# One conditioning row per stretch of half steps: moving w_ada passes on VectorE, and four more SwiGLU pairs transposed by DMA

## The chip, the cores and the metric

The kernel runs on one core of a Trainium2 chip. The metric is the device time of one execution in microseconds, as a median of several runs; the kernel before takes 2384.58 us (three runs, 2383.78 to 2389.31).

## The reference, cut to what matters

One decoder layer over 256 tokens of width 2048, in float32:

```python
mod = (silu(c) @ w_ada + b_ada).reshape(9, 2048)       # conditioning: shift, scale, gate, three times
h = modulate(rms_norm(x, norm_ffn1), mod[0], mod[1])
x = x + 0.5 * mod[2] * swiglu(h, w_ffn1_gu, w_ffn1_down)         # d_ff 5632
h = modulate(rms_norm(x, norm_mix), mod[3], mod[4])
x = x + mod[5] * token_mixing(h, w_in, w_ret_branch, w_swa_branch, w_out, sinks)
h = modulate(rms_norm(x, norm_ffn2), mod[6], mod[7])
x = x + 0.5 * mod[8] * swiglu(h, w_ffn2_gu, w_ffn2_down)
return rms_norm(x, norm_final)
# token_mixing: h @ w_in (13312 columns) -> retention q, k, v, g | window attention q, k, v | two branch gates
#   out = (sigmoid(gate_ret) * (ro @ w_ret_branch) + sigmoid(gate_swa) * (so @ w_swa_branch)) @ w_out
```

The nine rows of `mod` are 9 x 2048 dot products of length 2048 with `silu(c)`. They are worked out on VectorE beside the matmuls of the layer.

## The kernel before, in words

**Products.** Every large matrix product is done on TensorE with float32 split into a high and a low part, three terms each: high by high, low by high, high by low (lines 338, 339 and 341). A weight block of four k-tiles by 512 columns (1 MB) is loaded by SyncE into a `raw` tile. It is used in two *half steps* of two k-tiles each. For a half step ScalarE casts the block's half to the high part `wh` (L351) and VectorE subtracts to get the low part `wl` (L353); then TensorE does 12 matmuls of 512 columns, for two token halves and two k-tiles. `wh` and `wl` have three buffers each (pool `wsp`), so they can be made at most three half steps ahead. Where the activations lie in float32 (the branches, the output projection and both down projections) ScalarE and VectorE also split an activation pair `a` for every two k-tiles (L386, L387).

**Raw tiles.** There are four (`RAWS = 4`). Weight blocks use them, and so do the rows of `w_ada`: a row of the conditioning is 128 outputs, a 1 MB tile of 128 by 2048.

**Conditioning.** A row is loaded (L201) and reduced in four passes of 512 columns (`ada_pass`, L206), each followed by a small read of the sum. `tick()` is called after each half step; it adds `pace["rate"]` and takes the next pass when one is due. In the mixer three outputs (7, 6 and 5: 48 rows, 192 passes) go at 0.95 passes per half step, and at 0.25 while the attention's softmax runs; in the second feed-forward output 8 (16 rows) goes at 64/160 = 0.4. A row's load is issued two passes ahead of its first. In the first feed-forward the rows go to a tile of their own (`slot`) for the most part.

**Order.** SyncE's queue follows the order of the code (`manual_schedule`), and it holds everything behind an instruction that waits, say for a free raw tile. The order on the other engines is set by the framework's scheduler at build time, except in the norm stages, which are written out by hand. `tc.issue_after(ins)` only forbids that an instruction stands ahead of `ins` on its engine.

**SwiGLU pairs.** The up projection of a feed-forward is done in eleven pairs of 512 columns (gate, up). A pair's product must be transposed. Either TensorE does it (`transpose_to`, L479, eight 128x128 transposes for a pair, copied out of PSUM at L480), or a DMA does: ScalarE takes the float32 words apart in two 16-bit planes (L496), SyncE issues a transposing DMA (L501), and ScalarE puts the planes together (L512). These three steps are generators (`later`) that advance once per weight block. In the first feed-forward the opening pairs are 0 to 7 (`EARLY = 8`); of these, pairs 1 and 5 go by DMA, and so do pairs 8 and 9; in the second, pairs 0 to 9.

**Softmax.** In the mixer, eight groups of four heads (quads) pass through `softmax_heads`, one step per weight block. ScalarE writes a quad's weights apart into `planes_of` (L1159), and four steps later SyncE issues two transposing DMAs for them (L1168), in the same queue as the weight loads.

Of the kernel before, what the change touches and what calls it, by code (L numbers as in the profile page):

```python
# [20 lines left out]
DFF = 5632  # L21
# [56 lines left out]
def layer_kernel(  # L78
# [164 lines left out]
    def conditioning(outputs, place, behind):  # L243
# [5 lines left out]
        for m, gain, row in outputs:  # L249
            sums = ada_sums()  # L250
            for k in range(KD):
                for q in range(AQ):
# [13 lines left out]
                            gate_out(m, row)  # L266
                    yield

    def gate_out(m, row):
# [77 lines left out]
    def split(pool, tag, src, n, hi_engine="act"):  # L347
        k = src.shape[1]
        hi = pool.tile([P, 2, n], F32R, tag=tag + "h", name=nm(tag + "h"))[:, :k, :]
        lo = pool.tile([P, 2, n], F32R, tag=tag + "l", name=nm(tag + "l"))[:, :k, :]  # L350
        cast.append(nc.scalar.copy(hi, src).ins)  # L351
        del cast[:-1]
        low.append(nc.vector.tensor_sub(lo, src, hi.bitcast(F32)).ins)  # L353
        del low[:-1]
        return hi, lo

    cast, low, newest = [], [], []
# [651 lines left out]
    for g, ks in enumerate(groups):  # L1009
        final = g == len(groups) - 1  # L1010
        if final:
            set_pace(ROWS_FFN1, 32 * 192 // 32, place_row, 1)
        order = chunks if (len(groups) - g) % 2 else chunks[::-1]
        coming = iter(()) if final else group(groups[g + 1])
        due = 0 if final else 2 * len(groups[g + 1])
        stay = () if final else order[-2:]
        for i, n in enumerate(order):
            visit(n, ks, n not in stay, final)
            if final:
                turn_step()  # L1020
            last = len(order) - 2
            for _ in range((i + 1) * due // last - i * due // last if i < last else i == last):
                next(coming, None)
            if n in stay:
                continue
            if not final:
                to_parts(n)
            elif n % 2:
                swiglu_up(
                    banks.pop(n - 1),  # L1030
                    banks.pop(n),
                    tiles,
                    n // 2,
                    (part_of(n - 1), part_of(n)),
                    n // 2 in (1, 5),
                )
    gate = gate_row()
    tiles.append(slot())
    row_ring.append(two_rows())
    pace["rate"] = (192 - 32) / 117  # L1040
    pace["ahead"] = AQ
    ffn_up(held, gu, tiles, EARLY, turned=range(EARLY, DFF // CH - 1))
    gate_in = gate_load(gate, 2)
    wi = w_in[0]
    held, head, ahead, *calls = into_norm(3, wi, O_SK, O_SV)
# [6 lines left out]
    soft = one.tile([P, NT * D], F32, tag="x", name="soft")  # L1052
    planes_of = one.tile([P, D], F32, tag="row", name="planes_of")
    RATE_SOFT, RATE_AFTER = 0.25, 0.95
    set_pace([(7, 2, None), (6, None, None), (5, None, 1.0)], 192 / 0.95, raw_row, 2)

    def in_chunk(c0):
        return gemm(held, wi, [c0])[0]
# [142 lines left out]
    def softmax_heads():  # L1201

        turned = {}
        for at in range(4 * (QUADS + 1) + 2):
# [15 lines left out]
        pace["rate"] = RATE_AFTER  # L1220

    for ci in range(4):
        b = in_chunk(O_SQ + ci * CH)
        work = []
        for t in range(NT):
            u = t512()
            nc.any.tensor_copy(u, b[t])
            work.append(turn_by_dma(qo[:, ci * 4 : ci * 4 + 4, t * P : (t + 1) * P], u))

        def asking(ci=ci):  # L1230
            asked.add(ci)
            if ci == 0:
                pace["rate"] = RATE_SOFT
                side.append(softmax_heads())

        soon(later(work, asking))
# [259 lines left out]
```

## Time and profile before

| what | value |
|---|---|
| median of three runs | 2384.58 us |
| profiled execution, its own time | 2393.78 us |
| its span | 2392.0 us |
| TensorE busy | 2351.4 us, 98% |
| VectorE busy | 1702.1 us, 71% |
| ScalarE busy | 1310.0 us, 55% |
| granted TensorE clock, mean | 0.997 |
| DMA queue that carries the loads (q1), share of 16 engines | 74.4% |

The page gives busy time by engine and by group of instructions. TensorE's busy time is modelled and overlaps, so the number of matmuls in a stretch of time says more than the busy share. In quiet minutes (60 us) 266 matmuls stand. The first feed-forward ends at about 760 us, the window attention's softmax runs from about 900 to 1080 us, the branch products from 1270 to 1530 us, the second feed-forward's up projection from about 1640 to 2140 us.

### The profile page before, as it was taken

Reading aid. Unit: us, or ns where it says so; the run is one execution under the profiler, and the core shown is the slowest. Engines: PE = TensorE matmul, PEld = TensorE weight load, DVE = VectorE, ACT = ScalarE, POOL = GpSimd, SP = SyncE. Lnnn points to the kernel's source line nnn. Section 1 sums busy time; section 2 is a strip of 40 time slices with the busy share of each in tenths; the row PEclk is TensorE's granted clock in tenths of the full one; section 3 lists DMA queues with packets and bytes.
Section 4 is the critical chain, followed back from the end, with each engine's and each line's share of the span. In section 5 each row is a group of like instructions: output and inputs, shape, how many; then the busy total and the mean of one; then the engine's idle time right before and its main releaser. Section 6 shows DMA issues by size and latency. Waiting matters only on the chain. (4 is left out here: it accounts for less than half of the span.)

```text
span 2392.0 us, 28418 instructions
## 1 busy us (share of the span) xinstructions
PE 2351.4 (98%) x10470; PEld 1924.5 (80%) x10470; DVE 1702.1 (71%) x2635; ACT 1310.0 (55%) x1792; POOL 7.7 (0%) x18
## 2 busy tenths in 40 slices
PE   7999999999999999999999999999999999999998
PEld 5788888888788888778887787887888888888886
DVE  6887799778877768976776676767655555545656
ACT  6553456454546568774555464466445445454544
POOL 0000000000000000000000000000000000000000
PEclk9999999999999999999999999999999999999999
DMA  9977789998876789867689797755667877765553
GB/s 354 367 278 277 265 284 342 349 339 316 321 255 236 279 270 247 253 213 286 248 278 293 236 299 282 272 195 192 237 238 237 254 247 246 255 220 194 183 204 124
DMA packets 177581, 625.78 MB, mean 262 GB/s; under 512 B 100321, under 2 KB 100705, under 8 KB 106913
## 3 DMA queue, kind: packets, MB, share of 16 engines
q1 hardware_dynamic: 175362, 613.11, 74.4%
q0 software_dynamic: 1504, 9.81, 1.0%
q8 instruction: 82, 1.34, 0.2%
q10 hardware_dynamic: 576, 1.05, 0.1%
q14 instruction: 57, 0.47, 0.1%
HBM read 597.16 MB, written 4.22 MB: 251 GB/s over the span
## 5 line engine op out<-in xcount | busy, mean ns | idle before, releaser
L351 ACT CAST wh<-raw 128x1024 fp32r<-128x1024 f32 x794 | 834.0, 1053 | 927.1 <-PE pa L339 895.4
L353 DVE TENSOR_TENSOR wl<-raw,wh 128x1024 fp32r<-128x1024 f32 x794 | 964.2, 1223 | 524.6 <-ACT wh L351 522.3
L338 PE MATMUL pa<-wh,hh 128*128 128x512 f32 x2192 | 855.4, 391 | 3.3 <-ACT wh L351 3.3
L339 PE MATMUL pa<-wh,hl 128*128 128x512 f32 x2192 | 854.5, 390 | 0.2 <-DVE hl L601 0.2
L341 PE MATMUL pa<-wl,hh 128*128 128x512 f32 x2192 | 778.2, 392 | 1.4 <-DVE wl L353 1.3
L338 PEld LDWEIGHTS pa<-wh,hh 128*128 128x128 f32 x2192 | 411.9, 188 | 93.6 <-ACT wh L351 5.3
L341 PEld LDWEIGHTS pa<-wl,hh 128*128 128x128 f32 x2192 | 409.9, 188 | 90.4 <-DVE wl L353 4.3
L339 PEld LDWEIGHTS pa<-wh,hl 128*128 128x128 f32 x2192 | 412.1, 188 | 85.2 <-DVE hl L601 0.4
L339 PE MATMUL pa<-wh,a 128*128 128x512 f32 x944 | 365.8, 390 | 0.4 <-DVE a L387 0.4
L341 PE MATMUL pa<-wl,a 128*128 128x512 f32 x944 | 351.0, 392 | 9.4 <-DVE wl L353 9.4
L338 PE MATMUL pa<-wh,a 128*128 128x512 f32 x944 | 350.7, 392 | 1.7 <-DVE t L607 1.1
L206 DVE CUSTOM_DVE_ANT_0 raw<-raw,cact 128x512 f32<-128x512 f32 (+1 forms) x296 | 189.8, 695 | 65.5 <-DMA raw<-in_w_ada_dram 59.4
L341 PEld LDWEIGHTS pa<-wl,a 128*128 128x128 f32 x944 | 177.3, 188 | 49.9 <-DVE wl L353 13.5
L338 PEld LDWEIGHTS pa<-wh,a 128*128 128x128 f32 x944 | 178.0, 189 | 40.3 <-DVE t L607 1.9
L339 PEld LDWEIGHTS pa<-wh,a 128*128 128x128 f32 x944 | 177.8, 188 | 37.9 <-DVE a L387 1.0
L206 DVE CUSTOM_DVE_ANT_0 slot<-slot,cact 128x512 f32<-128x512 f32 (+1 forms) x216 | 170.0, 835 | 5.1 <-DMA slot<-in_w_ada_dram 4.8
L512 ACT COPY slot<-back 128x512 uint16<-128x512 uint16 x124 | 82.7, 766 | 0.0
L387 DVE TENSOR_TENSOR a<-slot,a 128x512 fp32r<-128x512 f32 x118 | 80.5, 684 | 0.0
L386 ACT CAST a<-slot 128x512 fp32r<-128x512 f32 x118 | 72.7, 617 | 1.9 <-DVE t L671 1.9
L496 ACT COPY flat<-t 128x512 uint16<-128x512 uint16 x112 | 63.5, 616 | 8.1 <-DVE t L1344 5.5
L206 DVE DVE_READ_ACCUMULATOR2_ANT sums<- 128x1 f32 x512 | 42.2, 82 | 0.0
L996 DVE TENSOR_TENSOR slot<-slot,pa 128x512 f32<-128x512 f32 x48 | 31.9, 683 | 3.2 <-PE pa L341 3.1
(205 smaller groups left out, 1143.1 us busy)
## 6 DMA issues: line engine op xcount, KB each, us to landing
raw<-in_w_ffn_gu_dram SPq DMA_DIRECT2D x160, 1024.0 KB, 5.2
raw<-in_w_in_dram SPq DMA_DIRECT2D x104, 1024.0 KB, 5.7
raw<-in_w_ffn_down_dram SPq DMA_DIRECT2D x88, 1024.0 KB, 4.9
raw<-in_w_ada_dram SPq DMA_DIRECT2D x73, 1024.0 KB, 5.5
slot<-in_w_ada_dram SPq DMA_DIRECT2D x67, 1024.0 KB, 7.1
raw<-in_w_ffn_gu_dram SPq DMA_DIRECT2D x32, 512.0 KB, 5.5
raw<-in_w_swa_branch_dram SPq DMA_DIRECT2D x16, 1024.0 KB, 5.1
raw<-in_w_ret_branch_dram SPq DMA_DIRECT2D x16, 1024.0 KB, 5.0
```

The source lines that it names most:

```text
L206: nc.vector.tensor_tensor_reduce(out=w[:, at], in0=w[:, at], in1=cact[:, at], scale=1.0, scalar=0.0, op0=ALU.mult, op1=ALU.add, accum_out= ...
L338: nc.tensor.matmul(ps, ah[:, j, ts], wh[:, j, :], start=first, stop=False)
L339: nc.tensor.matmul(ps, al[:, j, ts], wh[:, j, :], start=False, stop=False)
L341: nc.tensor.matmul(ps, ah[:, j, ts], wl[:, j, :], start=False, stop=last).ins
L351: cast.append(nc.scalar.copy(hi, src).ins)
L353: low.append(nc.vector.tensor_sub(lo, src, hi.bitcast(F32)).ins)
L386: nc.scalar.copy(hi, v)
L387: nc.vector.tensor_sub(lo, v, hi.bitcast(F32))
L496: nc.scalar.copy(planes[:, i, :], words(src)[:, :, i])
L512: nc.scalar.copy(into[:, :, :, i], held["turned"][:, i])
L996: nc.vector.tensor_add(p, p, b)
```

## The change

Three things are changed.

1. The conditioning of the mixer (outputs 7, 6, 5) and of the second feed-forward (output 8) goes through a new generator, `conditioning_by_rows`. It paces rows and not passes: `share` is added per half step, and when 4 have come together the next row's load is issued. Its four passes follow in four consecutive half steps, beginning three half steps after the load (`lead=3`). Each pass is put behind a low part on VectorE: `low[0]`, the one traced before the latest, since `split` now keeps two. The shares are 0.95, 0.25 and 0.4, as the rates were.
2. Of the opening pairs, 1, 3, 5 and 7 go by DMA and not only 1 and 5.
3. The eleventh pair (number 10) goes by DMA in both feed-forwards.

```diff
+    def conditioning_by_rows(outputs, behind, lead=3):
+        sums = {}
+        coming = [(m, k, gain, row) for m, gain, row in outputs for k in range(KD)]
+        queue, now, due = [], 0, AQ
+        while coming or queue:
+            due += pace["share"]
+            if due >= AQ and coming:
+                due -= AQ
+                m, k, gain, row = coming.pop(0)
+                raw = raw_row()
+                ada_load(m, k, raw)
+                pin = behind.ins if behind is not None and now < AQ else None
+                queue.append([m, k, gain, row, raw, now + lead, 0, pin])
+            if queue and queue[0][5] <= now:
+                m, k, gain, row, raw, _, q, pin = queue[0]
+                if m not in sums:
+                    sums[m] = ada_sums()
+                with tc.issue_after(pin or low[0]):
+                    ada_pass(k, raw, sums[m], q)
+                queue[0][6] += 1
...
+            now += 1
+            yield
...
         low.append(nc.vector.tensor_sub(lo, src, hi.bitcast(F32)).ins)
-        del low[:-1]
+        del low[:-2]
...
-                    n // 2 in (1, 5),
+                    n // 2 % 2 == 1,
...
-    ffn_up(held, gu, tiles, EARLY, turned=range(EARLY, DFF // CH - 1))
+    ffn_up(held, gu, tiles, EARLY, turned=range(EARLY, DFF // CH))
...
-    set_pace([(7, 2, None), (6, None, None), (5, None, 1.0)], 192 / 0.95, raw_row, 2)
+    set_pace_by_rows([(7, 2, None), (6, None, None), (5, None, 1.0)], RATE_AFTER)
...
-    set_pace([(8, None, 0.5)], 160, raw_row, 2)
-    ffn_up(held, w_ffn2_gu[0], tiles, 0, head, range(DFF // CH - 1), ahead)
+    set_pace_by_rows([(8, None, 0.5)], 0.4)
+    ffn_up(held, w_ffn2_gu[0], tiles, 0, head, range(DFF // CH), ahead)
```

In the program as a whole TensorE has 32 transposes fewer, ScalarE has 16 copies apart (L496) and 16 copies together (L512) more, 8 copies out of PSUM (L480) and 2 others (L1197) fewer, VectorE 2 copies more, and SyncE 8 transposing DMAs more. Lines of the changed kernel lie 35 further down.

The order on VectorE in the branch products (about 1358 us of the profile before). `wl` is a low part, `a` the low half of an activation pair, and an L206 pair of rows is one pass and the read of its sum. Before, where the pass and its read stand four times in a row at the first "...":

```order
L353 TENSOR_TENSOR wl_10680<-raw_10660,wh_10679 128x1024
L206 ISA raw_10778,sums_10735<-raw_10778,cact 128x512
L206 ISA sums_10735 128x1
...
L353 TENSOR_TENSOR wl_10701<-raw_10698,wh_10700 128x1024
L387 TENSOR_TENSOR a_10657<-slot_9563,a_10657 128x512
L353 TENSOR_TENSOR wl_10720<-raw_10698,wh_10719 128x1024
L353 TENSOR_TENSOR wl_10746<-raw_10743,wh_10745 128x1024
```

The same place in the changed kernel:

```order
L388 TENSOR_TENSOR wl_10703<-raw_10700,wh_10702 128x1024
L206 ISA raw_10638,sums_9299<-raw_10638,cact 128x512
L206 ISA sums_9299 128x1
L422 TENSOR_TENSOR a_10661<-slot_9566,a_10661 128x512
L388 TENSOR_TENSOR wl_10722<-raw_10700,wh_10721 128x1024
L206 ISA raw_10638,sums_9299<-raw_10638,cact 128x512
L206 ISA sums_9299 128x1
L223 TENSOR_REDUCE modc<-sums_9299 128x16
L224 TENSOR_TENSOR modc<-modc,bcols 128x16
L388 TENSOR_TENSOR wl_10747<-raw_10744,wh_10746 128x1024
L206 ISA raw_10718,sums_10781<-raw_10718,cact 128x512
```

Four passes in one piece between two low parts have become one pass after each low part.

SyncE's loads there, first before:

```order
L328 DMA raw_10698<-in_w_ret_branch_dram 128x2048
L328 DMA raw_10743<-in_w_ret_branch_dram 128x2048
L201 DMA raw_10778<-in_w_ada_dram 128x2048
L328 DMA raw_10781<-in_w_ret_branch_dram 128x2048
L328 DMA raw_10822<-in_w_ret_branch_dram 128x2048
```

and after:

```order
L201 DMA raw_10638<-in_w_ada_dram 128x2048
L363 DMA raw_10664<-in_w_ret_branch_dram 128x2048
L363 DMA raw_10700<-in_w_ret_branch_dram 128x2048
L201 DMA raw_10718<-in_w_ada_dram 128x2048
L363 DMA raw_10744<-in_w_ret_branch_dram 128x2048
```

The new row `raw_10718` is loaded while the passes of `raw_10638` are still to come (they stand after the low parts of `raw_10664` and `raw_10700`), so two of the four raw tiles hold rows there, and the weight blocks take turns on the other two. Before, the row `raw_10778` is read in one piece, ahead of the low parts of `raw_10698` and `raw_10743`, two blocks that stand before it in the queue of loads.

ScalarE in the softmax (about 950 us), where `planes_of` is the quad's copy that the transposing DMAs wait for. Before:

```order
L351 CAST wh_7509<-raw_7507 128x1024
L1159 COPY planes_of<-soft 128x768 x4
L351 CAST wh_7526<-raw_7507 128x1024
L512 COPY slot_6360<-back_7395 128x4x128 x2
L512 COPY slot_6360<-back_7443 128x4x128 x2
L351 CAST wh_7589<-raw_7587 128x1024
```

After, a few casts further on:

```order
L386 CAST wh_7613<-raw_7595 128x1024
L531 COPY flat_7554<-t_7500 128x512 x2
L386 CAST wh_7644<-raw_7642 128x1024
L1194 COPY planes_of<-soft 128x768 x4
L531 COPY flat_7631<-t_7507 128x512 x2
L386 CAST wh_7660<-raw_7642 128x1024
L386 CAST wh_7688<-raw_7686 128x1024
```

This quad's four copies stand after the 317th weight cast before and after the 321st now, two casts ahead of that of the block `raw_7686`. On SyncE the quad's two transposing DMAs stand directly ahead of the load of `raw_7686`, as they did before. A second quad, sixteen casts later, has moved in the same way (from after the 333rd cast to after the 337th).

More of the change, by code (lines that the diff above doesn't have):

```diff
@@ L267, in conditioning, with set_pace_by_rows @@
                     yield
+    def conditioning_by_rows(outputs, behind, lead=3):
[18 more added lines that the diff above has]
+                queue[0][6] += 1
+                if q == AQ - 1:
+                    queue.pop(0)
+                    if k == KD - 1:
+                        ada_end(m, slice(0, KD), sums[m], gain)
+                        if row is not None:
+                            gate_out(m, row)
+            now += 1
+            yield
+    def set_pace_by_rows(outputs, share):
+        assert next(pace["steps"], None) is None
+        pace["steps"] = conditioning_by_rows(outputs, pace["behind"])
+        pace["rate"], pace["due"], pace["share"] = 1.0, 0.0, share
     def gate_out(m, row):
@@ L1219, in softmax_heads @@
             yield
-        pace["rate"] = RATE_AFTER
+        pace["share"] = RATE_AFTER
     for ci in range(4):
@@ L1232, in asking @@
             if ci == 0:
-                pace["rate"] = RATE_SOFT
+                pace["share"] = RATE_SOFT
                 side.append(softmax_heads())
```

## The prediction

> **What bounds the kernel now.** I read the page first, then TensorE by minutes, then what it waits for, then VectorE at one of the waits.
>
> ```profile
> PE 2351.4 (98%) x10470; PEld 1924.5 (80%) x10470; DVE 1702.1 (71%) x2635; ACT 1310.0 (55%) x1792; POOL 7.7 (0%) x18
> L351 ACT CAST wh<-raw 128x1024 fp32r<-128x1024 f32 x794 | 834.0, 1053 | 927.1 <-PE pa L339 895.4
> ```
>
> TensorE is the bound. ScalarE's weight casts idle 927.1 us, 895.4 of it until TensorE gives a buffer back: operands usually lie ready up to three half steps ahead, so only a delay longer than that lead costs time. The minutes show where this happens (after the stretch: TensorE's busy time and number of matmuls; the granted clock stands before the DMA share).
>
> ```profile
> 1260.00:1320.00 60.00, 57.57 (x250) 46.36 (x249) 41.11 (x70) 37.22 (x49) 0.00 (x0) 1.00 1.00 291
> 1320.00:1380.00 60.00, 54.94 (x224) 43.84 (x224) 43.77 (x74) 26.24 (x32) 0.00 (x0) 0.94 0.71 250
> 1380.00:1440.00 60.00, 60.00 (x266) 49.67 (x266) 45.00 (x73) 36.74 (x46) 0.00 (x0) 1.00 0.89 285
> 1440.00:1500.00 60.00, 58.17 (x257) 47.82 (x256) 38.98 (x64) 25.84 (x29) 0.00 (x0) 1.00 0.79 294
> 1500.00:1560.00 60.00, 59.45 (x262) 48.50 (x261) 42.22 (x63) 28.91 (x34) 1.05 (x2) 1.00 0.73 260
> 1860.00:1920.00 60.00, 59.74 (x264) 49.17 (x263) 32.97 (x40) 28.83 (x34) 0.00 (x0) 1.00 0.81 254
> ```
>
> A quiet minute has 266 matmuls, so one takes 60/266 = 0.2256 us and a half step of twelve 2.71 us. The two minutes of the first branch products lack 58 matmuls, those of the second 13: 71 x 0.2256 = 16.0 us. 1860 to 1920 lacks 2, 0.45 us. The waits of TensorE between 1270 and 1540 us (total, times, longest) name VectorE:
>
> ```profile
> PE pa L341 <- DVE wl L353: 8.9, 8, 2.2
> PE pa L338 <- DVE slot L1360: 0.4, 1, 0.4
> PE pa L339 <- DVE a L387: 0.4, 1, 0.4
> ```
>
> The waits are 9.7 us of the 16.0; the rest is restart and the clock, below. SyncE and VectorE ahead of the wait at 1360.9:
>
> ```profile
> 1349.35 0.33 SPq L201 DMA_DIRECT2D raw<-in_w_ada_dram  x1
> ```
>
> ```profile
> 1353.37 1.23 DVE L353 TENSOR_TENSOR wl<-raw,wh 128x1024 fp32r<-128x1024 f32 x1 [0.89 <-ACT wh L351]
> 1357.13 0.69 DVE L206 CUSTOM_DVE_ANT_0 raw<-raw,cact 128x512 f32<-128x512 f32 x1 [2.53 <-DMA raw<-in_w_ada_dram]
> ...
> 1359.59 1.22 DVE L353 TENSOR_TENSOR wl<-raw,wh 128x1024 fp32r<-128x1024 f32 x1
> 1360.72 0.68 DVE L387 TENSOR_TENSOR a<-slot,a 128x512 fp32r<-128x512 f32 x1
> 1361.33 1.22 DVE L353 TENSOR_TENSOR wl<-raw,wh 128x1024 fp32r<-128x1024 f32 x1
> ```
>
> The row lands 7.8 us after its issue. VectorE stands 2.53 us at its first pass, then does four passes (2.46 us from 1357.13 to 1359.59), and the low part that TensorE needs stands behind all of it: 6.2 us from low part to low part where TensorE uses one every 2.71.
>
> **Part 1, the passes in the mixer.** Nothing is added: the same 192 passes at 0.61 us. In the new order one pass follows each low part. Low part 1.14 us (start to start, 1359.59 to 1360.72), pass 0.61, activation pair 0.61 every second half step: 2.06 us of 2.71, so VectorE keeps up at every half step. The row's wait goes too: the load is issued three half steps ahead, and the pass stands behind low parts whose blocks are queued after the row, so the data needed next by TensorE no longer waits for a row that comes later. I take the whole 16.0 us (bounds: 9.7 if only the waits shrink, 16.0). In the second feed-forward the same gives 0.4 us, and there a row comes only every ten half steps. The mixer's last row ends some nine half steps (24 us) later than before by the order, still some eighteen ahead of the additions that need its gate: nothing waits for it.
>
> Around the first feed-forward's down projection the scheduler has moved a group of passes behind the additions that free PSUM. TensorE waited there at 645 us:
>
> ```profile
> PE pa L338 <- DVE t L607: 1.1, 2, 0.6
> ```
>
> These 1.1 us may go, but the low part behind the passes comes as late as before, so I count 0 (bounds: 1.1 us gained to 1.1 lost).
>
> The stage's clock is in those 16 us. The two stretches behind the longest waits:
>
> ```profile
> 1323.00:1326.80 3.80, 3.80 (x11) 2.94 (x12) 1.56 (x3) 1.11 (x2) 0.00 (x0) 0.57 0.91 319
> 1361.30:1364.60 3.30, 3.30 (x9) 2.61 (x8) 1.24 (x2) 0.49 (x1) 0.00 (x0) 0.52 0.94 348
> ```
>
> The clock is granted at 0.57 and 0.52 for about 3.5 us after waits of 2.0 to 2.2 us: 20 matmuls in 7.1 us, where 31 would fit, 2.5 us lost. A new wait of 2 us therefore has to be priced with up to 1.3 us on top. The Trainium skill (TensorE: Matmul & The Clock Gate, HAM oscillation) says that idle gaps over about 3.4 us are what brings the clock down; here 2.0 to 2.2 us were enough, so the measurement decides, and by the page's figure the new waits below would carry no such addition.
>
> **Part 2, the transposes.** Four pairs leave TensorE: 32 transposes. One pair on TensorE:
>
> ```profile
> 316.57 0.39 PE L338 MATMUL pa<-wh,hh 128*128 128x512 f32 x1
> 316.80 1.03 PE L479 MATMUL ps<-small_c,t 128*128 128x128 f32 x8
> 317.59 0.48 PE L341 MATMUL pa<-wl,hh 128*128 128x512 f32 x1
> ```
>
> Eight take 317.59 - 316.80 = 0.79 us of a TensorE that has no other gap there: 4 x 0.79 = 3.2 us gained. What they cost elsewhere:
>
> ```profile
> L512 ACT COPY slot<-back 128x512 uint16<-128x512 uint16 x124 | 82.7, 766 | 0.0
> L496 ACT COPY flat<-t 128x512 uint16<-128x512 uint16 x112 | 63.5, 616 | 8.1 <-DVE t L1344 5.5
> ```
>
> ```profile
> 336.19 1.69 SPq L501 DMA_TRANSPOSE back<-flat  x1
> 342.71 3.39 SPq L501 DMA_TRANSPOSE back<-flat  x1
> ```
>
> A pair takes four copies of each kind, 4 x (0.766 + 0.616) = 5.5 us on ScalarE, spread over some nine weight blocks (49 us) of an engine that is 55% busy, and holds SyncE 1.7 to 3.4 us for each tile. Pair 1 does this at 336 to 346 us without a wait of TensorE, since all loads there run ahead; the new pairs lie in the same stage, and the eleventh at the start of a down projection that needs it in its last block group, 10 x 4 half steps or 108 us later. I take 0 (bounds: 0 to 1 us a pair).
>
> **Part 3, the raw tiles.** This speaks against the change. A row now holds its raw tile from load to last pass, 3 + 4 = 7 half steps, and rows come every 4/0.95 = 4.2, so mostly two of four tiles hold rows and weight blocks take turns on two. A block's load then starts when the block before last is finished, and loop time is landing + cast + two low parts with a pass and a pair between. In the mixer from 1090 to 1540 us the median landing times are:
>
> ```profile
> raw<-in_w_in_dram SPq DMA_DIRECT2D x45, 1024.0 KB, 5.0
> raw<-in_w_ada_dram SPq DMA_DIRECT2D x35, 1024.0 KB, 6.0
> raw<-in_w_ret_branch_dram SPq DMA_DIRECT2D x15, 1024.0 KB, 5.0
> back<-flat SPq DMA_TRANSPOSE x12, 7.5
> ```
>
> The loop is 5.0 + 1.05 + 1.14 + 0.61 + 0.61 + 1.22 and about 0.1 for signals = 9.7 us for four half steps of 10.8: 1.1 us to spare, besides the lead. Single landings as long as the 7.8 us above overdraw it by 1.7 us and are made good in two loops. I take 1.5 us in all, near the median's end (bounds: 0; 71 us if every landing took 7.8, 42 loops x 1.7). The Trainium skill (DMA: Bandwidth & Descriptors, Anatomy of one DMA) fits 2.0 us + bytes/436e3, an estimate of 4.4 us for 1 MB; by it this term would be 0, the sum 1.5 us lower.
>
> **Part 4, the softmax.** Two quads' copies now stand four casts later on ScalarE, two casts ahead of a block whose load waits on SyncE behind the quad's transposes. Before, the closest case has three casts:
>
> ```profile
> 1028.06 1.06 ACT L351 CAST wh<-raw 128x1024 fp32r<-128x1024 f32 x1
> 1029.02 3.03 ACT L1159 COPY planes_of<-soft 128x768 uint16<-128x768 uint16 x4
> 1031.95 1.05 ACT L351 CAST wh<-raw 128x1024 fp32r<-128x1024 f32 x1
> 1034.80 1.06 ACT L351 CAST wh<-raw 128x1024 fp32r<-128x1024 f32 x1 [1.79 <-PE pa L339]
> 1039.80 1.05 ACT L351 CAST wh<-raw 128x1024 fp32r<-128x1024 f32 x1 [3.95 <-DMA raw<-in_w_in_dram]
> ```
>
> From the end of the first cast (1029.12) to that of the late one (1040.85) are 11.7 us. With three buffers a cast ends about 1.05 us into the half step two before its own. The cast two later must be done within 4 x 2.71 - 1.05 = 9.8 us, so TensorE waits 1.9 us; three later it was within 12.5, and it did not wait. Two places: 3.8 us (bounds: 0, if small products stretch those half steps; 6.4 with 1.3 us of half clock at each).
>
> **Sum.** 2393.78 (the profiled execution's own time; its span is 2392.0) - 16.0 - 0.4 - 3.2 + 1.5 + 3.8 = 2379.5 us. The median of the runs, 2384.58, lies 9.2 us below the profiled execution. I carry this difference over unchanged: 2370 us.
>
> **The rivals.**
> - *The two-tile loop becomes the bound* (slower). The same number of bytes moves as before, which speaks against it; that loads are no longer drawn ahead speaks for it. Without this term the gain is 19.6 - 3.8 = 15.8 us over 42 loops, 0.38 us each: the gain is gone once landings average 5.0 + 1.1 + 0.38 = 6.5 us, the row's own 6.0 not far. At 7.0 us: 42 x 0.9 = 38 us, less 15.8, 2407 us.
> - *The stalls are in part the profile's*. The difference of 9.2 us could be these very waits, longer when transfers are traced. Then the runs gain only 14.3 - 9.2 = 5.1 us: 2379.5.
> - *The wait stays.* The row still lands after its pass comes up, and VectorE stands before each low part: only the block of passes is gone. Of the 6.2 us above, 2.53 were the wait, 41%. Keeping 41% of 16.0 leaves 14.3 - 6.6 = 7.7 us: 2377, with any lateness of the loads near 2382. Against it: the load is issued 8.1 us ahead and rows have a free tile then.
>
> **How the numbers follow.** Forecast 0.70, two-tile loop 0.12, profile's stalls 0.10, the wait stays 0.08. 0.3% of 2384.58 is 7.2 us, about what a measurement of this kernel can tell from no change: faster is below 2377.4, slower above 2391.7. The forecast is faster; of the two rivals near the edge 0.03 falls there too; the rest of them, 0.15, is the same; the loop is slower. The range: without any new wait 2370 - 5.3 = 2365, and if runs lost as much again at places not counted here (3.7 us), 2361; upwards it takes in the second and third rival, to 2384, and leaves out the loop.
>
> **What would show it.** Right: in the branch stage no four passes in a row on VectorE, no wait of TensorE over 1 us, clock 1.00, 264 or more matmuls in each minute; 32 transposes at the transposing line instead of 64 in the feed-forwards; weight loads released by low parts, casts that wait for DMA for up to 1 us. Two waits of about 2 us on a cast held by a load, at about 960 and 1010 us. Wrong: casts waiting for DMA throughout 1090 to 1540 us with landings over 6.5 us; waits of VectorE for row loads still at 2 us; new waits of TensorE at 400 to 540 us behind the added transposes.

## The result, and the profile after

The changed kernel takes 2392.08 us (median, 2387.27 to 2396.61), the kernel before 2384.93 us (2383.47 to 2389.31): a ratio of 1.0027, 95% interval 1.0020 to 1.0035. It is 7.15 us slower, 0.3%, where 2370 was forecast and faster; the difference is small, but the interval of the ratio leaves out 1. The profiled execution took 2392.35 us (span 2390.6), close to its median.

The page of the changed kernel, TensorE's counts and the weight casts:

```profile
PE 2349.6 (98%) x10438; PEld 1919.6 (80%) x10438; DVE 1706.7 (71%) x2637; ACT 1322.1 (55%) x1814; POOL 7.7 (0%) x18
L386 ACT CAST wh<-raw 128x1024 fp32r<-128x1024 f32 x794 | 832.3, 1053 | 915.6 <-PE pa L374 812.1
```

32 matmul instructions are gone. Of the casts' idle time all but 812.1 us, that is 103.5 us, ends with something other than TensorE; before it was 31.7 (927.1 - 895.4). TensorE by minutes in the changed kernel (busy time and number of matmuls, granted clock, DMA share, GB/s):

```profile
600.00:660.00 60.00, 57.56 (x247) 0.97 0.77 291
840.00:900.00 60.00, 58.27 (x263) 1.00 0.89 274
900.00:960.00 60.00, 59.64 (x293) 1.00 0.71 208
960.00:1020.00 60.00, 58.45 (x287) 1.00 0.81 230
1020.00:1080.00 60.00, 57.61 (x276) 1.00 0.79 251
...
1260.00:1320.00 60.00, 58.01 (x253) 1.00 0.90 277
1320.00:1380.00 60.00, 59.39 (x260) 1.00 0.83 304
1380.00:1440.00 60.00, 58.21 (x250) 0.97 0.88 286
1440.00:1500.00 60.00, 59.78 (x264) 1.00 0.78 286
1500.00:1560.00 60.00, 59.78 (x264) 1.00 0.78 277
1860.00:1920.00 60.00, 60.00 (x267) 1.00 0.76 259
```

The minute from 1320 to 1380, at 224 matmuls and a clock of 0.94 before, is nearly full, and so is 1860 to 1920. But 1380 to 1440, full before, lacks 16, and the minutes of the softmax (960 to 1080) have 563 where the kernel before had 297 + 292 = 589. What ScalarE waits for between 1090 and 1540 us (total, times, longest):

```profile
ACT wh L386 <- PE pa L374: 147.2, 102, 2.4
ACT wh L386 <- DMA raw<-in_w_in_dram: 26.8, 8, 8.0
ACT wh L386 <- DMA raw<-in_w_swa_branch_dram: 10.0, 4, 4.0
ACT wh L386 <- DMA raw<-in_w_ret_branch_dram: 6.2, 3, 2.8
```

Casts now stand 43 us for weight loads. The same view of the kernel before names no load; there VectorE's passes waited 39.5 us for rows, and that wait is gone. The new order on VectorE is as the diff says, a pass (L206) behind each low part (L388):

```profile
1354.16 0.69 DVE L422 TENSOR_TENSOR a<-slot,a 128x512 fp32r<-128x512 f32 x1
1355.00 1.23 DVE L388 TENSOR_TENSOR wl<-raw,wh 128x1024 fp32r<-128x1024 f32 x1 [0.15 <-ACT wh L386]
1356.14 0.69 DVE L206 CUSTOM_DVE_ANT_0 raw<-raw,cact 128x512 f32<-128x512 f32 x1
```

So the trouble that was named is cured, and another has come. Where it is worst in the mixer, at 1423.4 us, SyncE's queue and the cast that TensorE then waits for read so:

```profile
1410.18 0.33 SPq L201 DMA_DIRECT2D raw<-in_w_ada_dram  x1
1410.56 5.01 SPq L536 DMA_TRANSPOSE back<-flat  x2
1415.67 1.01 SPq L363 DMA_DIRECT2D raw<-in_w_in_dram  x2
```

```profile
1422.34 2.00 ACT L386 CAST wh<-raw 128x1024 fp32r<-128x1024 f32 x2 [7.99 <-DMA raw<-in_w_in_dram]
```

A row's load and two transposing DMAs, which hold SyncE 5 us, stand ahead of two weight loads. The cast waits 7.99 us, nearly the whole lead of three half steps (8.1 us); with its own 1.05 us it takes more, and TensorE waits 1.8 us.

### The profile page after: what moved, and what is told of

The parts are those of the page before. It is cut to its first block, busy times and chain, and to the rows that moved or that the text cites. A ratio compares the mean times of both kernels' runs of the same rounds, so it can differ in the third digit from the quotient of the medians.

```text
span 2390.6 us, 28350 instructions
## 1 busy us (share of the span) xinstructions
PE 2349.6 (98%) x10438; PEld 1919.6 (80%) x10438; DVE 1706.7 (71%) x2637; ACT 1322.1 (55%) x1814; POOL 7.7 (0%) x18
## 3 DMA queue, kind: packets, MB, share of 16 engines
q10 hardware_dynamic: 576, 1.05, 0.1%
## 4 chain that ended last, share of the span: by engine, by line
PE 52%; DMA 2%; DVE 1%; ACT 1%; issue 0%; SPq 0%; DVEq 0%; ACTq 0%
PE pa L376 17%; PE pa L373 17%; PE pa L374 17%; DMA raw<-in_w_in_dram 1%; DVE wl L388 1%; ACT wh L386 1%; DMA back<-flat 0%; SPq L536 0%; PE ps L1228 0%; ACT flat L531 0%; PE pd L1327 0%; PE pd L1312 0%; PE pd L1326 0%; PE pd L1325 0%; DVE a L422 0%
## 5 line engine op out<-in xcount | busy, mean ns | idle before, releaser
L388 DVE TENSOR_TENSOR wl<-raw,wh 128x1024 fp32r<-128x1024 f32 x794 | 968.2, 1223 | 584.7 <-ACT wh L386 583.0
L386 ACT CAST wh<-raw 128x1024 fp32r<-128x1024 f32 x794 | 832.3, 1053 | 915.6 <-PE pa L374 812.1
L373 PEld LDWEIGHTS pa<-wh,hh 128*128 128x128 f32 x2192 | 411.9, 188 | 97.5 <-ACT wh L386 10.5
L206 DVE CUSTOM_DVE_ANT_0 raw<-raw,cact 128x512 f32<-128x512 f32 (+1 forms) x296 | 202.7, 693 | 10.0 <-ACT cact L173 6.1
L206 DVE CUSTOM_DVE_ANT_0 slot<-slot,cact 128x512 f32<-128x512 f32 (+1 forms) x216 | 170.0, 835 | 2.3 <-DMA slot<-in_w_ada_dram 2.2
L547 ACT COPY slot<-back 128x512 uint16<-128x512 uint16 x140 | 93.5, 766 | 0.0
L531 ACT COPY flat<-t 128x512 uint16<-128x512 uint16 x128 | 72.5, 616 | 3.8 <-DVE t L1300 3.7
L206 DVE DVE_READ_ACCUMULATOR2_ANT sums<- 128x1 f32 x512 | 42.6, 83 | 0.0
```

The lines of the kernel that those rows point to most:

```text
L206: nc.vector.tensor_tensor_reduce(out=w[:, at], in0=w[:, at], in1=cact[:, at], scale=1.0, scalar=0.0, op0=ALU.mult, op1=ALU.add, accum_out= ...
L373: nc.tensor.matmul(ps, ah[:, j, ts], wh[:, j, :], start=first, stop=False)
L531: nc.scalar.copy(planes[:, i, :], words(src)[:, :, i])
L547: nc.scalar.copy(into[:, :, :, i], held["turned"][:, i])
```

## The experiments

All of them compute the whole layer. Each is compared with runs of the kernel before on the same chip, and those medians moved by 1 us (2384.4 to 2385.3), so the table gives the difference too. The last columns count matmuls in the profiled execution. "Losses" in the expectations are worked out from the trace: the time from one 512-column matmul's start to the next matmul's beyond 0.227 us, summed where it is over 0.14 us (the next matmul may be of any size).

| kernel | median us | less before, us | 95% interval of the ratio | 960 to 1080 | 1260 to 1560 |
|---|---|---|---|---|---|
| before, the first profile | 2384.93 | 0 | | 589 | 1259 |
| before, second profile (e1) | | | | 590 | 1294 |
| changed | 2392.08 | +7.2 | 1.0020 to 1.0035 | 563 | 1291 |
| changed again (e6) | 2392.55 | +8.1 | 1.0027 to 1.0055 | 560 | 1305 |
| four pairs only (e2) | 2382.88 | -2.2 | 0.9983 to 1.0004 | 589 | 1303 |
| mixer's rows only (e3) | 2387.70 | +2.6 | 1.0002 to 1.0019 | 569 | 1310 |
| second feed-forward's rows only (e4) | 2387.86 | +2.8 | 0.9993 to 1.0014 | 590 | 1284 |
| pairs and mixer's rows (e5) | 2389.81 | +5.4 | 1.0013 to 1.0034 | 562 | 1304 |
| lead of 1 (e7) | 2381.75 | -2.7 | 0.9979 to 0.9997 | 566 | 1327 |
| lead of 5 (e8) | 2426.31 | +41.9 | 1.0169 to 1.0197 | 592 | 1183 |
| lead of 1, shift (e9) | 2381.56 | -3.8 | 0.9976 to 0.9994 | 579 | 1329 |
| shift (e10) | 2381.47 | -3.9 | 0.9976 to 0.9993 | 590 | 1315 |
| eleventh pair back (e11) | 2389.58 | +4.2 | 1.0009 to 1.0027 | 567 | 1283 |
| lead of 1, shift, pair back (e12) | 2381.02 | -4.3 | 0.9975 to 0.9992 | 578 | 1330 |
| shift in the softmax only (e13) | 2385.62 | +1.2 | 0.9993 to 1.0014 | 590 | 1296 |
| shift in the mixer only (e14) | 2387.28 | +2.9 | 1.0004 to 1.0022 | 563 | 1318 |
| shift, no added pairs (e15) | 2382.24 | -2.2 | 0.9980 to 0.9998 | 591 | 1313 |
| shift of eight (e16) | 2383.81 | -0.6 | 0.9992 to 1.0012 | 585 | 1309 |

**The kernel before, profiled once more.** No edit.

> The kernel before once more, for a second profiled execution. If the 9.2 us by which its first profiled execution lay above the median were stalls of the branch products in that one execution, the new one has fewer: own time 2383 to 2388 us, matmuls missing from the minutes 1260 to 1380 and 1440 to 1560 us at 20 to 45 and not 71, no half clock. If profiling always costs that much: own time 2392 to 2395 us and again some 70 missing.

It took 2387.34 us, in the range that meant that the first profile's stalls were in part its own. TensorE in that second profile of the kernel before:

```profile
1260.00:1320.00 60.00, 56.77 (x247) 1.00 0.99 287
1320.00:1380.00 60.00, 57.82 (x253) 1.00 0.79 283
1380.00:1440.00 60.00, 60.00 (x267) 1.00 0.88 288
1440.00:1500.00 60.00, 59.97 (x265) 1.00 0.78 288
1500.00:1560.00 60.00, 59.45 (x262) 1.00 0.72 258
```

In the four minutes of which the prediction counted 71 missing matmuls, 37 are missing here (1064 - 247 - 253 - 265 - 262): 8.3 us, and no half clock. So only about half of the 16.0 us was there to be had. Two experiments below leave the mixer as it was, e2 and e4: ScalarE, VectorE and SyncE go through the same instructions in the same order from 660 to 1560 us as in the kernel before. They lack 27 and 46 matmuls from 1260 to 1560 us, so the first profile, with 71, is the worst of four.

**The parts, one at a time.** e2 has the four pairs alone:

```diff
-                    n // 2 in (1, 5),
+                    n // 2 % 2 == 1,
...
-    ffn_up(held, gu, tiles, EARLY, turned=range(EARLY, DFF // CH - 1))
+    ffn_up(held, gu, tiles, EARLY, turned=range(EARLY, DFF // CH))
...
-    ffn_up(held, w_ffn2_gu[0], tiles, 0, head, range(DFF // CH - 1), ahead)
+    ffn_up(held, w_ffn2_gu[0], tiles, 0, head, range(DFF // CH), ahead)
```

> The kernel before with the four more pairs turned by DMA alone. Theory A (rows that hold raw tiles cost the time): 32 transposes less on TensorE, 3 us faster than before, 2382 us. Rival B (the added transposing DMAs hold SyncE and the weight loads behind them): 3 to 10 us slower than before.

2382.88 us, 2.2 less than the kernel before in that comparison, near theory A's 2382; the interval just holds no change.

e3 and e4 have `conditioning_by_rows` in the mixer alone and in the second feed-forward alone (the `set_pace_by_rows` line of the one or the other in the change's diff, no added pairs).

> The kernel before with the new generator in the mixer alone. Theory A: the whole loss lies here, 10 us slower than before (2395), casts that wait for weight loads 35 us or more between 1090 and 1540 us as in the changed kernel. Rival B: no slower than before, 2380 to 2385.

> The kernel before with the new generator in the second feed-forward alone. There weight loads keep three tiles or more, so theory A expects no difference: within 1 us of before. If the pinning behind low parts itself cost time, it would show here as 2 us or more.

The mixer's rows gave 2387.70 us, 2.6 more than before, between the two expectations and not the gain that the prediction had there. By the counts the loss is at the softmax (21 matmuls fewer than in e1, 4.7 us), not in the branches. The second feed-forward's rows gave 2387.86; the interval holds no change, so it can't tell 0 from the 2 us of that expectation. The three differences add up to +3.2 us where the whole change has +7.2.

**Together, and once more.** e5 is the change without the second feed-forward's rows, e6 the changed kernel itself.

```diff
-    set_pace_by_rows([(8, None, 0.5)], 0.4)
+    set_pace([(8, None, 0.5)], 160, raw_row, 2)
```

> The whole change without the second feed-forward's rows. Alone, the turned pairs gave 2382.9 and the mixer's rows 2387.7, against 2385.1 for the kernel before. Theory S (the parts add up, and the 7 us of the whole change are an accident of the runs that measured it): 2385.1 - 2.2 + 2.6 = 2385.5, 2384 to 2387. Theory I (turned pairs and the mixer's rows spoil each other): 2390 to 2392, with waits of the matmuls near 891, 1311 and 1423 us as in the changed kernel. Theory F (the second feed-forward's rows are what costs in company): below 2386, and the rest of the 7 us comes back with them.

> The changed kernel unaltered. If the loss belongs to the kernel: 2391 to 2393 again. If it belongs to the chip or the runs that measured it: 2385 to 2388. For the profiled execution: the waits at 972 to 978 and 1026 to 1032 us (quads of the softmax) must come again, 5 us together, under either; the wait at 1423 us (1.8 us and half clock behind it) comes again if it is set by the order of the loads, and doesn't if it hangs on one late landing.

e5 took 2389.81 us, 5.4 above before, where -2.2 + 2.6 make 0.4: pairs and rows of the mixer do not seem to add up, though each of the three differences is only known to some 2 us. The pairs don't change any order in the mixer: from 660 to 1560 us ScalarE, VectorE and SyncE go through the same instructions in the same order in e3 and e5. What they spoil for the rows is a matter of timing, and it isn't settled. e6 took 2392.55, so the loss is the kernel's. Its trace has the waits of the softmax again (5.2 us of losses), those at 645, 891 to 927 and 1312 us, and the one at 1423 us too, without half clock.

**How long a row holds its tile.** e7 and e8 load a row one and five half steps ahead of its first pass.

```diff
-    def conditioning_by_rows(outputs, behind, lead=3):
+    def conditioning_by_rows(outputs, behind, lead=1):
```

> The whole change, but a row is loaded one half step ahead of its first pass and not three, so that it holds its raw tile for two half steps less. Theory T (rows hold the raw tiles, so the mixer's weight loads are issued late and casts wait for them): the casts' waits for landings between 1090 and 1540 us fall from 43 us to below 25, the matmuls' losses between 1240 and 1570 us from 7.7 to below 4, the time to 2386 to 2389. Theory Q (the softmax's quads and the passes' place in VectorE's order are the cost): the time stays within 1.5 us of the changed kernel's, the losses between 960 and 1100 us stay at 5 us.

> The whole change, but a row is loaded five half steps ahead of its first pass. Theory T: the casts' waits for landings between 1090 and 1540 us rise from 43 us to above 70, the matmuls' losses between 1240 and 1570 us from 7.7 to above 12, the time to 2397 or more. Theory Q: within 1.5 us of the changed kernel's.

e7: 2381.75 us, 10.8 less than the changed kernel in the same comparison and faster than the kernel before. e8: 2426.31 us. ScalarE's waits between 1090 and 1540 us, first of e7:

```profile
ACT wh L386 <- PE pa L374: 178.3, 121, 2.4
ACT wh L386 <- DMA raw<-in_w_in_dram: 10.0, 4, 3.6
```

Then of e8, with the median landing times of that stretch behind them:

```profile
ACT wh L386 <- DMA raw<-in_w_in_dram: 60.6, 20, 9.5
ACT wh L386 <- DMA raw<-in_w_swa_branch_dram: 26.6, 12, 5.2
```

```profile
raw<-in_w_in_dram SPq DMA_DIRECT2D x49, 1024.0 KB, 6.2
raw<-in_w_swa_branch_dram SPq DMA_DIRECT2D x15, 1024.0 KB, 6.6
```

Casts waited 11.5 us for loads with a lead of 1 (10.0, and 1.5 at a second kind of weights), 43 with 3, and 92 with 5 (60.6, 26.6 and 4.5 at the third kind). The mixer's 1330 quiet matmuls came to 1327, 1291 and 1183. Theory T is right in direction. In e8 a row holds its tile for nine half steps and one comes every 4.2, so rows hold more than two tiles of four; weight landings are 6.2 to 6.7 us. But e7 gained more than T said (2386 to 2389), and the next runs show that the lead is not all.

**Where the rows stand.** e10 keeps the lead of 3 and only adds 1.0 to what has come together when the softmax starts. There, at 0.25 per half step, it brings the rows four half steps forward; in the mixer behind it, at 0.95, the same 1.0 is one half step. e9 does it with a lead of 1.

```diff
-            due += pace["share"]
+            due += pace["share"] + pace.pop("shift", 0.0)
...
-                pace["share"] = RATE_SOFT
+                pace["share"], pace["shift"] = RATE_SOFT, 1.0
```

> A row is loaded one half step ahead of its first pass, and with the softmax's start the rows come four half steps earlier, so that a row's load stands ahead of the quad's two turning transfers in SyncE's queue, as in the kernel before, and not two weight loads behind them. One half step alone gave 2381.75. Theory S (the quads lose because the rows stand at the wrong place of a quad's turn): the losses between 960 and 1100 us fall from 4.7 to below 1.5, the time to 2377 to 2379. Theory B (four passes in consecutive half steps are too much beside a quad wherever they stand): the losses stay above 4, the time at 2381 to 2383.

> The changed kernel, three half steps of lead kept, with that shift of the softmax's rows alone. Theory S: the losses between 960 and 1100 us fall from 5 to below 1.5, those between 1240 and 1570 us stay at 5 to 8, the time is 2387.5 to 2389.5. Theory B: 2391 to 2393.

e10: 2381.47 us. Without any shorter hold of the tiles, 11 us less than the changed kernel, more than the quads alone could give. TensorE in e10:

```profile
960.00:1020.00 60.00, 60.00 (x297) 1.00 0.85 249
1020.00:1080.00 60.00, 60.00 (x293) 1.00 0.74 218
...
1380.00:1440.00 60.00, 59.47 (x261) 1.00 0.84 281
```

The quads' waits are gone and the mixer's are smaller. Yet casts stood longer for weight loads between 1090 and 1540 us than in the changed kernel, 52 us against 43 (37.2, 10.5 and 4.3):

```profile
ACT wh L386 <- DMA raw<-in_w_in_dram: 37.2, 13, 6.7
```

So the sum of these waits isn't the price. At the place of 1423 us what counts is the longest one against the 8.1 us by which operands lie ready: 8.0 us in the changed kernel, 7.6 in e6 and 6.7 in e10, and TensorE waits 1.8, 1.5 and 0.5 us behind them. SyncE at the first of the two quads, in the changed kernel:

```profile
957.97 3.29 SPq L1203 DMA_TRANSPOSE a<-planes_of  x2
961.32 1.39 SPq L363 DMA_DIRECT2D raw<-in_w_in_dram  x2
962.80 0.38 SPq L201 DMA_DIRECT2D raw<-in_w_ada_dram  x1
963.94 0.33 SPq L363 DMA_DIRECT2D raw<-in_w_in_dram  x1
964.32 6.89 SPq L536 DMA_TRANSPOSE back<-flat  x1
```

And in e10:

```profile
954.91 1.75 SPq L1203 DMA_TRANSPOSE a<-planes_of  x1
956.75 7.61 SPq L363 DMA_DIRECT2D raw<-in_w_in_dram  x3
964.41 1.24 SPq L536 DMA_TRANSPOSE back<-flat  x1
```

In the changed kernel the row's load stands between the weight loads behind a quad's two transfers; in e10, as in the kernel before, ahead of these transfers. The weight loads go out 4.6 us earlier there, though at the wait near 926 us, which both have, the two executions are within 1 us of each other.

But the row's load is not all that has moved. SyncE follows the order of the code; ScalarE's order is made anew at each build, and in e10 the quads' copies stand elsewhere too. Counted in the traces (which of the weight casts a quad's copies follow, third and fifth quad):

| copies follow cast | kernels | losses from 960 to 1100 us |
|---|---|---|
| 321 and 337 | changed, e3, e5, e6, e7, e11, e14 | 3.6 to 5.6 us |
| 317 or 318, and 333 or 334 | before, e1, e2, e4, e8, e10, e13, e15, e16 | 0.2 to 1.1 us |
| 317 and 333, and a lead of 1 | e9, e12 | 2.3 us, at the fourth and sixth quad |

e8 speaks for one of the two. It has the rows' loads at the same places of SyncE's queue as the changed kernel, two weight loads behind a quad's transfers, but the copies nearly where the kernel before has them, and these quads lose nothing. Its first quad has moved instead (from cast 301 to 305), and there TensorE waits 4.8 us at 931 us. So it is the place of the copies on ScalarE that goes with the loss, as the prediction's part 4 had it, and not the place of the row's load in SyncE's queue. No run moved the copies alone, and e8's longer lead sets it apart in other places. The half steps of e16's expectation are the same thing: counted from the copies, which release a quad's transfers and with them the loads behind, two weight loads of the changed kernel have one half step before their first low part, two of e16 have two, and none behind a quad in e10 has under four. The raw tiles would leave each of them three or more. In the mixer it is the tiles that leave two half steps for most loads, in both kernels.

With a lead of 1 the shift gave nothing (e9 2381.56, e7 2381.75), where theory S had promised 3 us or more; the time is theory B's, and the losses of 2.3 us lie between the two. Matmuls between 960 and 1080 us rise by 13 (566 to 579), but between 900 and 960 they fall from 293 to 282.

**The quads or the mixer.** e13 takes the shift back when the softmax ends (`pace["shift"] = -1.0` beside `pace["share"] = RATE_AFTER`); e14 shifts only from there on (`1.0` there, none at the start), by one half step.

> The shift by four half steps when the softmax starts, taken back when it ends: the quads as in the kernel that is shifted throughout (2381.5), the mixer's rows behind them where the changed kernel has them. Theory Q (nearly all of the 11 us lies at the quads): losses between 960 and 1100 us below 1.5, time 2382 to 2384. Theory M (the place of the rows decides in the mixer too): losses between 960 and 1100 us below 1.5, but 5 or more between 1240 and 1570 us (the changed kernel had 4.8 and 7.3), time 2385 to 2388.

> The other half: no shift in the softmax, the shift when it ends. Theory Q: the quads still lose 5 us, time 2388 to 2391. Theory M: the quads still lose 5 us, the losses between 1240 and 1570 us fall to 3 or less, time 2386 to 2388. If most of the gain was neither: 2383 or less.

Against the kernel before of the same comparison the changed kernel stands at +8.1 us (e6), e13 at +1.2, e14 at +2.9, e10 at -3.9. The shift in the softmax is worth 6.9 us, that in the mixer 5.2, and both together 12.0: they add up, as far as differences known to 2 or 3 us can tell. Both times lie in theory M's ranges, and the losses say the same: 0.4 us at the quads and 7.2 between 1240 and 1570 us in e13, 4.7 and 2.2 in e14. In e13 the copies stand after casts 318 and 333, in e14 after 321 and 337, so the 6.9 us are those of the copies' places as well. The matmuls: 960 to 1080 us 590 in e13 and 563 in e14; 1260 to 1560 us 1296 in e13 and 1318 in e14. The minute with the wait at 1423 us, e13 and then e14:

```profile
1380.00:1440.00 60.00, 57.85 (x249) 0.97 0.83 270
```

```profile
1380.00:1440.00 60.00, 59.94 (x264) 1.00 0.84 287
```

SyncE at that place has the same order in the changed kernel, e13, e14 and e10: a row's load, two transposing DMAs, two weight loads. What differs is how long the row's load waits for the last pass of an older row, which still holds the tile (`sums` is the read behind a pass), with the queue standing behind it. From 1395 to 1420 us, in the changed kernel and then in e14:

```profile
SPq L201 <- DVE sums L206: 5.8, 2, 3.9
SPq L201 <- DVE sums L206: 0.6, 3, 0.2
```

The longest such wait is 5.0 us in e13 and 0.2 in e10. The shift changes VectorE's and ScalarE's order in the mixer too, so that this wait is the cause fits all four traces but isn't shown by itself.

e15 undoes the added pairs in e10 (the lines of e2 the other way round), and e16 doubles the shift (`2.0`).

> Rows in the mixer and the second feed-forward with the shift, but the four pairs turned by TensorE as before. If the pairs and the rows add up once the quads are right: 2381.5 + 2.2 = 2383.7, 2383 to 2385. If the pairs still spoil something for the rows: below 2382.

> The shift doubled, eight half steps: the row's load stands three loads ahead of the quad's turning transfers. Two weight loads of the softmax then have two half steps between the release of their raw tile and their first low part (one in the changed kernel, four with the shift by four). Theory R (that slack decides): losses between 960 and 1100 us of 1 to 4, time 2382 to 2386. Theory P (only the order of the row's load and the quad's transfers decides): below 1, time 2381 to 2382.

e15: 2382.24 us, between the two expectations. Against before the pairs are worth 3.9 - 2.2 = 1.7 us on top of well placed rows, which can't be told from their 2.2 alone. e16: 2383.81 us, with losses of 0.9 us between 960 and 1100 us. The time lies in theory R's range and the losses just below it; theory P has the losses right and the time some 2 us too low. e8 above speaks against P: there the order of the row's load and the quad's transfers is the changed kernel's, and the third and fifth quad lose nothing.

**The eleventh pair.** e11 is the changed kernel with the first feed-forward's eleventh pair on TensorE again, e12 the same with a lead of 1 and the shift.

```diff
-    ffn_up(held, gu, tiles, EARLY, turned=range(EARLY, DFF // CH))
+    ffn_up(held, gu, tiles, EARLY, turned=range(EARLY, DFF // CH - 1))
```

> The changed kernel with the first feed-forward's eleventh pair turned by TensorE again. The wait of 2.4 us at 645 us must go and the three shorter ones of the kernel before (2.0 us) come back. If the change's step at 645 us costs what the trace shows (4.0 against 2.0) and the transposes are worth 0.8: 1.2 us less than the changed kernel, 2391 if that is 2392.3. If the half clock behind the wait is a matter of chance: the same within 1 us.

> One half step of lead, the shift, and the first feed-forward's eleventh pair by TensorE. By the sum of what the runs show (2381.75, less 4 for the quads under theory S, plus 0.2 at 645 us where the changed kernel of that lead lost 2.6 without half clock): 2377 to 2379, and the same within 1 us as the kernel with both but that pair. Under theory B 2381 to 2383.

e11 took 2389.58 us, about 3 us less than the changed kernel, where 1.2 were expected; the two intervals overlap. The minute from 600 to 660 us has 256 matmuls again, as before, not 247; and the two from 840 to 960 us have 568 and not 556, some 2.7 us, though the pair is long done by then. Where the rows stand there as in the changed kernel, the stretch loses with the eleventh pair and not without it (e5, with it, has 553; e3, without it, 569; e2, with the pair and the old rows, 567), and the order on ScalarE, VectorE and SyncE is the same there in the changed kernel and in e11. Why it feels the pair isn't settled. e12 took 2381.02 us, the lowest median here, in theory B's range and not in that of S. e7, e9, e10 and e12 lie within 0.8 us of each other and can't be told apart; all are faster than both the kernel before (ratio of e12 0.9984, 0.9975 to 0.9992) and the changed one.

## Why the prediction was wrong

Two terms failed. The price of part 1, -16.0 us, was twice what another execution of the same kernel had to give (8.3 us). And part 3, +1.5 us, was too small: the mixer lost 5.6 to 8.8 us in new stalls, the longest of them behind a late weight load, about as much as the passes' stalls that went. Part 4 was right in kind and too small, and two places that the prediction put at nothing cost 4.5 us.

**Part 1, -16.0 us in the mixer: mis-sized, and then lost again.** The mechanism held: no four passes stand in a row, no low part waits behind a row, and 1320 to 1380 us went from 224 matmuls at a clock of 0.94 to 260 at 1.00. Two things were wrong. The price came from one execution, and its stalls were twice an ordinary one's (71 and 37 missing matmuls). The prediction saw that this execution lay 9.2 us above the median and carried the difference over to the changed kernel; those 9.2 us were for the most part the stalls that it removed (34 matmuls or 7.7 us more than in the second profile), as its second rival said with a chance of 0.10. Tracing wasn't the reason, as that rival had it: the second profile is traced too and has half of them. And little of what was left was gained: 36 matmuls are missing from 1260 to 1560 us in the second profile of before, 39 and 25 in the two of the changed kernel. That is between 0.7 us lost and 2.5 us gained. By all traces with the one or the other order of the mixer it is 71, 36, 27 and 46 (before, e1, e2, e4) against 39, 25, 20, 26 and 47 (changed, e6, e3, e5, e11): on average 3 us gained, 1 us without the first profile, and the two groups overlap.

**Part 3, the raw tiles, +1.5 us: the step that failed in the mixer.** The loop was priced with median landings, and these were as expected (5.0 us for weights, 6.7 for rows in the changed kernel). The 4.4 us that the prediction set beside them from the Trainium skill (DMA: Bandwidth & Descriptors, Anatomy of one DMA) are a fit for DMAs issued through GpSimd; these loads go out from SyncE, and the medians measured here decide. But the chain has two terms that the loop left out: how long a row's load waits for its tile with the queue standing behind it, and how long transposing DMAs hold that queue ahead of weight loads. At 1410 us both come together (3.9 and 5.0 us). The matmuls missing in the mixer put all stalls left there at 5.6 to 8.8 us, and e13 against e10 shows 5.1 us of it gone when the rows come one half step earlier there. The rival of the two-tile loop had the right place; landings never had to reach 6.5 us on average for a loss, single waits near the 8.1 us by which operands lie ready were enough. Where the medians came near it (6.2 to 6.7 us in e8), the kernel took 34 us more: by the counts some 24 of them from 1260 to 1560 us, and 12 from 840 to 960 us.

**Part 4, the two quads, +3.8 us: right in place and kind, too small.** They came at 972 to 980 and 1026 to 1034 us. 26 matmuls fewer than before in these two minutes are 5.9 us, and by the times of e13 and e6 the quads cost 6.9 us. The prediction took one wait of 1.9 us for each quad; the trace has three, one at the late cast and two behind it. TensorE's waits from 960 to 1100 us in the changed kernel; the kernel before has none there:

```profile
PE pa L376 <- DVE wl L388: 2.6, 4, 1.0
PE pa L373 <- ACT wh L386: 1.3, 2, 1.1
```

That they come of the copies' four casts is borne out by the table of copies above: all seven traces with the copies there have the loss, the others have little of it, or 2.3 us at other quads.

**The down projection at 645 us, 0 with bounds of 1.1: outside its bounds.** One wait of 2.4 us took the place of three shorter ones, and half clock stood behind it: 247 matmuls against 256, 2.0 us. The wait in the changed kernel:

```profile
PE pa L376 <- DVE wl L388: 2.4, 1, 2.4
```

e2 has the wait without the rows, e3 keeps the old ones, and e11, which gives only the eleventh pair back to TensorE, hasn't got it: it belongs to that pair.

**Not foreseen: 840 to 960 us.** 556 matmuls against 271 + 296 = 567 before, 2.5 us, in both profiles of the changed kernel. Without the eleventh pair it is gone (e11, e3), with the pair and the old rows it isn't there (e2), and with a lead of 1 it is gone too (568 in e7); the cause stays open.

**Part 2, the transposes, -3.2 us: right, as far as e2's interval can tell.** The transposing line of the changed kernel:

```profile
L514 PE MATMUL ps<-small_c,t x32: 270/272/276, 315.5 to 383.4; 128*128 128x128 f32 x32
```

64 stood there. e2's -2.2 us is the 3.2, less 0.6 us of losses more at 645 us, and the rest is within its interval.

**The second feed-forward, -0.4 us:** 1860 to 1920 us is full, but the second profile of before has 267 there as well, so nothing was to be had.

The sum against the second profile of before: quads 27 matmuls or +6.1, 840 to 960 us +2.5, 645 us +2.0, mixer +0.7, transposes -3.2: +8.1 us, where the medians differ by 7.2. The two profiled executions themselves differ by 5.0 us (2392.35 - 2387.34), so some 3 us of the sum are made good at places not counted.

## What to carry to other kernels

Price a stall from more than one profiled execution: where the profile lies well above the median, the stalls that you mean to remove are the first suspects, and the difference must not be subtracted a second time. When a stream of background loads shares buffers and one in-order queue with the loads that feed the bound engine, price the single longest wait against the time by which operands lie ready, not the mean loop or the sum of waits: a load that waits for its buffer holds all loads behind it. Try the phase of such a stream before judging the idea; here the shift (four half steps in the softmax, one in the mixer) was worth 11 to 12 us, more than the change itself. And before such a gain is put down to the stream, compare the order on every engine: a scheduler that orders at build time had moved the softmax's copies as well, and their place goes with more than half of the gain.

## What was not expected of the hardware

The same wait of TensorE, 2.4 us at 645 us, is followed by half clock in some executions and not in others. 5.4 us behind it, in the changed kernel and then in e10 (matmuls, granted clock after POOL):

```profile
644.60:650.00 5.40, 5.40 (x17) 4.29 (x18) 5.40 (x13) 2.79 (x6) 0.00 (x0) 0.68 0.38 114
```

```profile
646.90:652.30 5.40, 5.39 (x24) 4.47 (x25) 5.40 (x13) 3.56 (x7) 0.00 (x0) 1.00 0.40 111
```

Seven matmuls or 1.6 us lie between them. Of the eleven traces with this wait, all of 2.43 to 2.45 us, four have the half clock (the changed kernel's two, e8 and e14). At 1423 us a wait of 1.8 us brought it and one of 1.5 us in e6 didn't; neither did one of 1.8 us in e16 (at 1305 us) nor one of 2.8 us in e4 (at 1491 us). The Trainium skill (TensorE: Matmul & The Clock Gate, HAM oscillation) has gaps of more than about 3.4 us as the condition; these traces have it after shorter ones, and not each time, so such a wait is worth a range (0 to 1.6 us here) and not a price.
